# Halved searches, a regrouped last sum of experts and a re-ordered last norm in a one-core transformer kernel

## The chip, the core and the metric

The kernel runs on one core of a Trainium2 chip. The metric is the device time of one execution in microseconds (us); times of a kernel are given as the median of several executions. The profile is that of one execution. The engines are TensorE (PE, with its weight loads as PEld), VectorE (DVE), ScalarE (ACT), GpSimd (POOL) and SyncE (SP), each with a queue of its own that is worked off in order; DMAs are issued from the queues of SP, ACT and POOL.

## The reference

Two residual blocks over 256 tokens of width 1024, in float32. The change lies in the second block's last part, a feed-forward layer with 16384 small experts (PEER), and in the norm that ends the model:

```
q = (hc @ w_query).reshape(B, T_CHUNK, PEER_HEADS, 2, PEER_DKEY // 2)
s = jnp.einsum('bthpd,hpnd->bthpn', q, sub_keys)
s_top, i_top = lax.top_k(s, PEER_TOPK)                 # 16 of 128 keys, for 8 heads and 2 halves
cand = s_top[..., 0, :, None] + s_top[..., 1, None, :]
g_s, pos = lax.top_k(cand, PEER_TOPK)                  # 16 of the pairs: an expert each
g = jax.nn.softmax(g_s, axis=-1)
act = jax.nn.gelu(jnp.einsum('btd,bthkd->bthk', hc, u_emb[e_idx]))
y = jnp.einsum('bthk,bthkd->btd', g * act, v_emb[e_idx])
...
x = x + g2[:, None, :] * y
return rms_norm(x, norm_final)     # x * rsqrt(mean(x*x) + EPS) * g
```

## The kernel before, in words

Tokens lie in two tiles of 128 (t = 0, 1), `xt[t]`; the normed input stands transposed in `hT`. Matmuls keep float32's precision with three passes: every operand is split into a high part, by ScalarE (`whi`, L157), and the rest, by VectorE (`wlo`, L137), and `mm3` (L207 to L209) multiplies high by high, low by high and high by low. The third pass is the one that needs `wlo`. Weights come through SP's queue into `raw`, in the fixed order of the list `items`; `nextw` hands out the next one and has the splits made two ahead in this part (`cfg["ahead"]` = 2).

The expert layer doesn't gather. It treats the 16384 experts as 128 groups of 128, here called experts 0 to 127. `s_step` makes the scores of one such expert for all tokens: 24 matmuls of 128x256 into the bank `sm`, in two halves of 12, then a gelu on ScalarE into `act`. A weight of each token for each expert is made as a product of one-hot matrices, and the sum over all experts is added up in four PSUM banks `po[t][h]`, h being the half of 512 columns. It runs in these stages:

- The key search. `top16` takes the 16 largest of each row with VectorE's MAX, MAX_INDEX and MATCH_REPLACE; one job is a block of 4 scores of 128 keys. Six of eight jobs run beside the query projections; the last two are the first thing in `route`. `route` is a generator that writes VectorE's work and yields a number after each piece. `keep_up` adds up these numbers and writes one `s_step` for each 1.6 of them behind the piece, so this sets the order in which `wlo` of the experts' weights stand between the pieces of VectorE's queue. Behind the route stand the transposes of its results `fl`.
- The one-hot blocks. 34 steps (`bt`) over 32 blocks of 8 tokens: `g_onehot` (VectorE: `oh` L1475, then the product `a` L1477), `g_mm` (PE, 24 matmuls, L1488) one step later, `g_out` (ScalarE, L1497). Some `s_step` are spread evenly over the steps; how many depends on how many were made in the route (`left`). Within a step the block's matmuls stand between the two halves of an `s_step`.
- The sum. `quanta` is the list of PE's work: remaining `s_step`, and for each expert n its two token tiles. `w_step(n)` multiplies scores by weights (VectorE `wf`, L1538) and splits the product (`wh` on ScalarE, L217, `wl` on VectorE, L218); it is written two experts ahead of its use. A tile of an expert is 6 matmuls of 128x512, three for each h.
- The end. `gated` multiplies a finished bank with the row `g2` and adds it to x (L1080, L1081 of `Gated`), then ScalarE sums the squares (L279). `rms` adds two sums (L1593) and GpSimd takes the power -0.5 (L1594). `give` multiplies x with this column and the norm's weight row `gf` in one VectorE instruction (L1598) and stores the half (L1599).

Of the kernel before, what the change touches and what calls it, by code (L numbers as in the profile page):

```python
# [9 lines left out]
F32 = mybir.dt.float32  # L10
# [4 lines left out]
AF = mybir.ActivationFunctionType  # L15
OP = mybir.AluOpType
# [3 lines left out]
P = 128  # L20
D = 1024
S = 256
NT = S // P
NEG = -1e30
USED = -3e38
EPS = 1e-6
# [3 lines left out]
NE = 128  # L30
# [30 lines left out]
def kernel(ctx: ExitStack, tc: tile.TileContext, A, LAY, stop=None):  # L61
    nc = tc.nc
    ctx.enter_context(tc.manual_schedule())
    V, ACT, G, PE = nc.vector, nc.scalar, nc.gpsimd, nc.tensor

    def pool(name, bufs=1, **kw):
        return tc.tile_pool(name=name, bufs=bufs, reuse_waits="tile", **kw)
# [5 lines left out]
    def pmm():  # L73
        return ps.tile([P, 512], F32, name="mm", tag="mm", bufs=4)
# [7 lines left out]
    def small(shape, name, dt=F32, bufs=4):  # L82
        return cst.tile(shape, dt, name=name, tag=name, bufs=bufs)

    def row(ap, n=D, eng=None):
        r = cst.tile([P, n], F32, name="grow", tag="grow", bufs=2)
        (eng or G).dma_start(r, bass.AP(tensor=ap.tensor, offset=ap.offset, ap=[[0, P], [1, n]]))
        return r
# [5 lines left out]
    xt = [cst.tile([P, D], F32, name=f"x{t}") for t in range(NT)]  # L94
# [70 lines left out]
    def nextw():  # L165
        while items[st["use"]][3] is not None:
            st["use"] += 1
        j = st["use"]
        ahead, k = 0, j + 1
        while k < len(items) and ahead < cfg["ahead"] and not cfg["spread"]:  # L170
            ahead += items[k][3] is None
            k += 1
        while st["split"] < k:
            split_one()
        while st["s"][j].lo is None:
            low_one()
        st["use"] += 1
        return st["s"].pop(j), items[j][1], items[j][2]
# [27 lines left out]
    def mm3(out, a, b, start, stop):  # L206
        PE.matmul(out, a[0], b[0], start=start, stop=False)  # L207
        PE.matmul(out, a[0], b[1], start=False, stop=False)  # L208
        PE.matmul(out, a[1], b[0], start=False, stop=stop)  # L209
# [68 lines left out]
    def sumsq(src, out, scale=1.0):  # L278
        ACT.activation(junk[:, :src.shape[1]], src, AF.Square, scale=scale, accum_out=out)  # L279
# [377 lines left out]
    for i in range(4):  # L657
        n = len(items)
# [24 lines left out]
    for x_ in seq:  # L683
        n = cnt[x_]
# [46 lines left out]
    for i in range(4):  # L731
        c, nk, _ = nextw()
# [133 lines left out]
    with pool("df") as sp:  # L866
# [3 lines left out]
        v = sp.tile([P, NT, D], F32, name="v")  # L870
        qx = sp.tile([P, 4, S], F32, name="xq")
        q = [sp.tile([P, 4, S], F32, name="q", tag=f"q{b}", bufs=1) for b in range(2)]
        k = [sp.tile([P, 4, S], F32, name="k", tag=f"k{b}", bufs=1) for b in range(2)]
# [403 lines left out]
    def top16(jobs):  # L1277

        for r in range(2):
            a, b = 8 * r, 8 * r + 8  # L1280
            for v_, i_, src in jobs:
                V.max(v_[:, a:b], src)  # L1282
            for v_, i_, src in jobs:
                V.max_index(i_[:, a:b], v_[:, a:b], src)  # L1284
            if r == 0:
                for v_, i_, src in jobs:
                    V.match_replace(src, v_[:, a:b], src, USED)  # L1287
# [72 lines left out]
    def s_step():  # L1360
        n = len(act)
        u, _, _ = nextw()
        p = psm()[:, :S]
        early = n % (AHEAD + 2) < FIRST
        act[n] = (dp if early else apool).tile([P, S], F32, name="act", tag="act", bufs=FIRST if early else AHEAD + 2 - FIRST)
        for k in range(8):
            mm3(p, u[:, k, :], hT[:, k, :], k == 0, k == 7)
            if k == 3:
                yield
        ACT.activation(act[n], p, AF.Gelu)  # L1370
        yield
# [8 lines left out]

    def route():
        for j_ in jobs:
            top16(j_)
            yield 4.0
        ib, gs, pos, fl = [], [], [], []
        for t in range(NT):
            ib.append(pq2.tile([P, 2, P, 2], BF16, name="ib", tag="ib", bufs=2))
# [28 lines left out]
            for s_ in range(2):  # L1416
                e = pq2.tile([P, 8, 16, 16], BF16, name="eq", tag="eq", bufs=2)
                V.tensor_tensor(e, io16[:, None].to_broadcast([P, 8, 16, 16]), pab[:, s_, :, None, :].to_broadcast([P, 8, 16, 16]),
                                op=OP.is_equal)
# [37 lines left out]
    for dt in route():  # L1457
        keep_up(dt)
# [62 lines left out]
    gpool = gst.enter_context(pool("gr"))  # L1521
    GW = {}

    def g_load(b):

        GW[b] = gpool.tile([P, NG, GI, GT], F32, name="G", tag="G", bufs=2)
        nc.scalar.dma_start(GW[b], gall[:, :, GI * GT * b:GI * GT * (b + 1)].rearrange("g p (i t) -> p g i t", t=GT))
# [5 lines left out]
    po = [[pmm() for h in range(2)] for t in range(NT)]  # L1533
    W = {}

    def w_step(n):
        wf = gpool.tile([P, S], F32, name="wf", tag="wf", bufs=3)
        V.tensor_tensor(wf.rearrange("p (g t) -> p g t", t=GT), act[n].rearrange("p (g t) -> p g t", t=GT), GW[n // GI][:, :, n % GI, :],  # L1538
                        op=OP.mult)
        W[n] = Split(gpool.tile([P, S], F32R, name="wh", tag="wh", bufs=3), gpool.tile([P, S], F32R, name="wl", tag="wl", bufs=3))  # L1540
        split_evac(W[n][:, :], wf)

    quanta = [("u", None)] * (2 * (AHEAD - len(act)))
    pos_ = AHEAD
    for n in range(NE):
# [2 lines left out]
            pos_ += 1  # L1548
        pos_ += 1
        quanta += [("v", (n, 0)), ("v", (n, 1))]  # L1550
    quanta[-4:] = [("v", (n, t, [h])) if t else ("v", (n, t)) for t, h in ((0, 0), (1, 0), (1, 1)) for n in (NE - 2, NE - 1)]
    vs = {}
    half = None
    for i, (kind, arg) in enumerate(quanta):
        if quanta[i + 1:i + 2] == [("v", (0, 0))]:
            w_step(0)
            w_step(1)
        if kind == "u":
            if half is None:
                half = s_step()  # L1560
                next(half)
            else:
                next(half)
                half = None
            continue
        n, t = arg[:2]
        if t == 0:
            if n == NE // 2:
                g2 = row(gdram[1], eng=nc.sync)
                gb2 = row(A["b_ada_2"][0, 5120:6144], eng=nc.sync)  # L1570
            if n == NE // 2 + 8:
                V.tensor_tensor(g2, g2, gb2, op=OP.add)
                gf = row(A["norm_final_2"], eng=nc.sync)
            vs[n], _, _ = nextw()
            if n + 2 < NE:
                w_step(n + 2)
            if n % GI == 1 and n // GI + 1 < NE // GI and n // GI:
                g_load(n // GI + 1)
        for h in arg[2] if t and len(arg) > 2 else range(2):
            mm3(po[t][h], W[n][:, t * P:(t + 1) * P], vs[n][:, 0, h * 512:(h + 1) * 512], n == 0, n == NE - 1)  # L1580
        if t and n < NE - 2:
            W.pop(n), vs.pop(n)

    gate = Gated(g2)
    fss = small([P, NT, 2], "ssn", bufs=2)
    fr = small([P, NT], "fr", bufs=1)

    def gated(t, h):
        gate(t, h, po[t][h])
        sumsq(xt[t][:, h * 512:(h + 1) * 512], fss[:, t, h:h + 1], D ** -0.5)  # L1590

    def rms(t):
        V.scalar_tensor_tensor(fr[:, t:t + 1], fss[:, t, :1], EPS, fss[:, t, 1:], op0=OP.add, op1=OP.add)  # L1593
        G.tensor_tensor(fr[:, t:t + 1], fr[:, t:t + 1], mhalf[:, :1], op=OP.pow)  # L1594

    def give(t, h):
        c = slice(h * 512, (h + 1) * 512)
        V.scalar_tensor_tensor(xt[t][:, c], xt[t][:, c], fr[:, t:t + 1], gf[:, c], op0=OP.mult, op1=OP.mult)  # L1598
        nc.sync.dma_start(A["out"][0, t * P:(t + 1) * P, c], xt[t][:, c])  # L1599

    for f in ((gated, 0, 0), (gated, 0, 1), (gated, 1, 0), (rms, 0), (gated, 1, 1), (give, 0, 0), (rms, 1), (give, 0, 1),
              (give, 1, 0), (give, 1, 1)):
        f[0](*f[1:])


# [66 lines left out]
def build(nc, arrays, lay, stop=None):  # L1672
    aps = {n: nc.dram_tensor(f"in_{n}_dram", a.shape, mybir.dt.from_np(a.dtype), kind="ExternalInput").ap()
           for n, a in arrays.items()}
    aps["out"] = nc.dram_tensor("out_0_dram", (1, S, D), F32, kind="ExternalOutput").ap()
    with tile.TileContext(nc) as tc:
        kernel(tc, aps, lay, stop)
# [11 lines left out]
```

## Time and profile before

| | us |
|---|---|
| median of 3 executions | 2079.52 (2077.22 to 2084.33) |
| the profiled execution | 2077.22 |
| its span | 2075.4 |
| PE busy in it | 2022.7 (97%) |
| VectorE busy | 1451.7 (70%) |
| ScalarE busy | 990.9 (48%) |

The span is what the profile covers; the execution's time has something around it. Times within a view count from the span's start. The search of the route begins at 1286.08, the one-hot blocks reach from 1400 to 1540, and the last update of x begins at 2062.98. [...]

### The profile page before, as it was taken

Reading aid. Unit: us, or ns where it says so; the run is one execution under the profiler, and the core shown is the slowest. Engines: PE = TensorE matmul, PEld = TensorE weight load, DVE = VectorE, ACT = ScalarE, POOL = GpSimd, SP = SyncE. Lnnn points to the kernel's source line nnn. Section 1 sums busy time; section 2 is a strip of 40 time slices with the busy share of each in tenths; the row PEclk is TensorE's granted clock in tenths of the full one; section 3 lists DMA queues with packets and bytes.
Section 4 is the critical chain, followed back from the end, with each engine's and each line's share of the span. In section 5 each row is a group of like instructions: output and inputs, shape, how many; then the busy total and the mean of one; then the engine's idle time right before and its main releaser. Section 6 shows DMA issues by size and latency. Waiting matters only on the chain. (4 is left out here: it accounts for less than half of the span.)

```text
span 2075.4 us, 34428 instructions
## 1 busy us (share of the span) xinstructions
PE 2022.7 (97%) x13678; PEld 1819.8 (88%) x13678; DVE 1451.7 (70%) x2280; ACT 990.9 (48%) x1524; POOL 41.7 (2%) x74
## 2 busy tenths in 40 slices
PE   8999999999999999999999899999999999999998
PEld 7999888998899798899978778999998888888886
DVE  6677566776577559766556879889976666666666
ACT  6444354444344445454444544455554444444443
POOL 2000000000000000000000000000000000000000
PEclk9999999999999999999999999999999999999999
DMA  7667545666576643365635343556676676776764
GB/s 277 208 249 251 180 146 192 237 241 238 189 252 231 235 156 121 124 213 195 211 117 175 102 162 114 182 175 231 244 255 216 209 231 208 226 251 212 230 212 135
DMA packets 142377, 416.92 MB, mean 201 GB/s; under 512 B 12468, under 2 KB 47428, under 8 KB 140040
## 3 DMA queue, kind: packets, MB, share of 16 engines
q1 hardware_dynamic: 102672, 372.04, 53.0%
q10 hardware_dynamic: 37976, 36.91, 5.6%
q0 software_dynamic: 1568, 5.77, 0.9%
q8 instruction: 107, 1.75, 0.3%
q14 instruction: 54, 0.44, 0.1%
HBM read 396.82 MB, written 17.86 MB: 200 GB/s over the span
## 5 line engine op out<-in xcount | busy, mean ns | idle before, releaser
L137 DVE TENSOR_TENSOR wlo<-raw,whi 128x1024 fp32r<-128x1024 f32 (+1 forms) x654 | 784.7, 1222 | 331.1 <-ACT whi L157 330.5
L157 ACT ACTIVATE whi<-raw 128x1024 fp32r<-128x1024 f32 (+1 forms) x654 | 666.2, 1048 | 134.7 <-PE mm L209 68.1
L209 PE MATMUL mm<-hT_hi,wlo 128*128 128x256 f32 x1680 | 472.1, 281 | 8.8 <-DVE wlo L137 8.8
L207 PE MATMUL mm<-hT_hi,whi 128*128 128x256 f32 x1680 | 477.9, 284 | 0.0
L208 PE MATMUL mm<-hT_lo,whi 128*128 128x256 f32 x1680 | 471.3, 281 | 0.0
L209 PEld LDWEIGHTS mm<-hT_hi,wlo 128*128 128x128 f32 x1680 | 316.5, 188 | 10.2 <-DVE wlo L137 10.2
L207 PEld LDWEIGHTS mm<-hT_hi,whi 128*128 128x128 f32 x1680 | 316.8, 189 | 6.2 <-issue 5.5
L208 PEld LDWEIGHTS mm<-hT_lo,whi 128*128 128x128 f32 x1680 | 316.8, 189 | 2.0 <-issue 1.9
L207 PE MATMUL sm<-hT_hi,whi 128*128 128x256 f32 (+1 forms) x1048 | 299.6, 286 | 4.3 <-DVE hT_hi L215 2.5
L209 PE MATMUL sm<-hT_hi,wlo 128*128 128x256 f32 (+1 forms) x1048 | 296.4, 283 | 4.3 <-DVE wlo L137 4.3
L208 PE MATMUL sm<-hT_lo,whi 128*128 128x256 f32 (+1 forms) x1048 | 296.3, 283 | 0.4 <-DVE hT_lo L218 0.4
L207 PEld LDWEIGHTS sm<-hT_hi,whi 128*128 128x128 f32 (+1 forms) x1048 | 199.2, 190 | 7.5 <-DVE hT_hi L215 2.9
L207 PE MATMUL mm<-whi,wh 128*128 128x512 f32 x512 | 202.6, 396 | 2.7 <-ACT wh L217 2.7
L209 PEld LDWEIGHTS sm<-hT_hi,wlo 128*128 128x128 f32 (+1 forms) x1048 | 199.2, 190 | 4.7 <-DVE wlo L137 4.7
L208 PE MATMUL mm<-wlo,wh 128*128 128x512 f32 x512 | 202.3, 395 | 0.0
L209 PE MATMUL mm<-whi,wl 128*128 128x512 f32 x512 | 202.2, 395 | 0.0
L208 PEld LDWEIGHTS sm<-hT_lo,whi 128*128 128x128 f32 (+1 forms) x1048 | 199.0, 190 | 3.0 <-DVE hT_lo L218 0.6
L217 ACT ACTIVATE wh<-wf 128x256 fp32r<-128x256 f32 x128 | 53.5, 418 | 215.2 <-DVE wf L1538 215.2
L207 PE MATMUL mm<-whi,gT_hi 128*128 128x512 f32 x352 | 139.9, 397 | 0.0
L209 PE MATMUL mm<-whi,gT_lo 128*128 128x512 f32 x352 | 139.1, 395 | 0.0
L208 PE MATMUL mm<-wlo,gT_hi 128*128 128x512 f32 x352 | 139.0, 395 | 0.0
L1370 ACT ACTIVATE act<-sm 128x256 f32<-128x256 f32 x128 | 49.1, 384 | 167.3 <-PE sm L209 167.2
(308 smaller groups left out, 2597.7 us busy)
## 6 DMA issues: line engine op xcount, KB each, us to landing
raw<-in_ffn_up_dram SPq DMA_DIRECT2D x176, 512.0 KB, 5.1
raw<-in_peer_u_dram SPq DMA_DIRECT2D x128, 512.0 KB, 3.9
raw<-in_peer_v_dram SPq DMA_DIRECT2D x128, 512.0 KB, 3.6
raw<-in_ffn_dn_dram SPq DMA_DIRECT2D x88, 512.0 KB, 5.1
raw<-in_w_ada_dram SPq DMA_DIRECT2D x48, 512.0 KB, 4.7
gall<-stage ACTq DMA_DIRECT2D x16, 1024.0 KB, 4.8
G<-gall ACTq DMA_DIRECT2D x16, 1024.0 KB, 7.2
raw<-in_diff_w_in_dram SPq DMA_DIRECT2D x28, 512.0 KB, 4.4
```

Source lines behind the costliest of these rows:

```text
L137: V.tensor_tensor(lo[:, :nk * w], r[:, :nk * w], c.hi.rearrange("p k w -> p (k w)").bitcast(F32), op=OP.subtract)
L157: ACT.activation(hi[:, :n], r[:, :n], AF.Copy)
L207: PE.matmul(out, a[0], b[0], start=start, stop=False)
L208: PE.matmul(out, a[0], b[1], start=False, stop=False)
L209: PE.matmul(out, a[1], b[0], start=False, stop=stop)
L217: ACT.activation(hi, src, AF.Copy)
L1370: ACT.activation(act[n], p, AF.Gelu)
```

## The change

The route searches each of its two blocks in two halves of two jobs and yields 2.8 after each half, where it yielded 4.0 after a whole one. The last three experts, not the last two, are summed by token tile: tile 0 of all three, then the first half of tile 1 of all three, then its second half. At the end, x is multiplied with the norm's weight in a step of its own (`gain`) before the column is known, and `give` only scales by the column, the first half of each tile on VectorE and the second on ScalarE. The order of the steps is written anew, and the products have three tiles of their own.

```diff
     def route():
         for j_ in jobs:
-            top16(j_)
-            yield 4.0
+            for k in range(0, 4, 2):
+                top16(j_[k:k + 2])
+                yield 2.8
...
-    quanta[-4:] = [("v", (n, t, [h])) if t else ("v", (n, t)) for t, h in ((0, 0), (1, 0), (1, 1)) for n in (NE - 2, NE - 1)]
+    quanta[-6:] = [("v", (n, t, [h])) if t else ("v", (n, t)) for t, h in ((0, 0), (1, 0), (1, 1)) for n in range(NE - 3, NE)]
...
-        if t and n < NE - 2:
+        if t and n < NE - 3:
             W.pop(n), vs.pop(n)
 
-    gate = Gated(g2)
-    fss = small([P, NT, 2], "ssn", bufs=2)
+    tmp = [gpool.tile([P, 512], F32, name="tmp", tag="tmp", bufs=3) for _ in range(3)]
+    fss = small([P, NT, 2], "ssf", bufs=1)
     fr = small([P, NT], "fr", bufs=1)
-
-    def gated(t, h):
-        gate(t, h, po[t][h])
-        sumsq(xt[t][:, h * 512:(h + 1) * 512], fss[:, t, h:h + 1], D ** -0.5)
+    parts = {(0, 0): (0, 512), (0, 1): (512, 512), (1, 0): (0, 512), (1, 1): (512, 512)}
+
+    def gated(t, k):
+
+        c, w = parts[t, k]
+        m, x_ = tmp[(2 * t + k) % 3][:, :w], xt[t][:, c:c + w]
+        V.tensor_tensor(m, po[t][c // 512][:, c % 512:c % 512 + w], g2[:, c:c + w], op=OP.mult)
+        V.tensor_tensor(x_, x_, m, op=OP.add)
+        sumsq(x_, fss[:, t, k:k + 1], D ** -0.5)
...
+    def gain(t, k):
+        c, w = parts[t, k]
+        V.tensor_tensor(xt[t][:, c:c + w], xt[t][:, c:c + w], gf[:, c:c + w], op=OP.mult)
 
     def give(t, h):
         c = slice(h * 512, (h + 1) * 512)
-        V.scalar_tensor_tensor(xt[t][:, c], xt[t][:, c], fr[:, t:t + 1], gf[:, c], op0=OP.mult, op1=OP.mult)
+        if h:
+            ACT.activation(xt[t][:, c], xt[t][:, c], AF.Copy, scale=fr[:, t:t + 1])
+        else:
+            V.tensor_scalar(xt[t][:, c], xt[t][:, c], fr[:, t:t + 1], None, op0=OP.mult)
         nc.sync.dma_start(A["out"][0, t * P:(t + 1) * P, c], xt[t][:, c])
 
-    for f in ((gated, 0, 0), (gated, 0, 1), (gated, 1, 0), (rms, 0), (gated, 1, 1), (give, 0, 0), (rms, 1), (give, 0, 1),
-              (give, 1, 0), (give, 1, 1)):
+    for f in ((gated, 0, 0), (gated, 0, 1), (gain, 0, 0), (rms, 0), (gain, 0, 1), (gated, 1, 0), (give, 0, 0), (give, 0, 1),
+              (gated, 1, 1), (gain, 1, 0), (rms, 1), (gain, 1, 1), (give, 1, 0), (give, 1, 1)):
         f[0](*f[1:])
```

On VectorE, the first of the two searches of the route stood as follows before (`v` and `i` are the values and indices found, `sc` the scores):

```order
L1282 MAX v_12418<-sc 128x8 x4
L1284 MAX_INDEX i_12420<-v_12418,sc 128x8 x4
L1287 MATCH_REPLACE sc<-v_12418,sc 128x128 x4
L1282 MAX v_12418<-sc 128x8 x4
L1284 MAX_INDEX i_12420<-v_12418,sc 128x8 x4
L137 TENSOR_TENSOR wlo<-raw,whi 128x1024 x3
```

and in the changed kernel VectorE has in the same place, up to the end of the first half and its splits:

```order
L1282 MAX v_12418<-sc 128x8 x2
L1284 MAX_INDEX i_12420<-v_12418,sc 128x8 x2
L1287 MATCH_REPLACE sc<-v_12418,sc 128x128 x2
L1282 MAX v_12418<-sc 128x8 x2
L1284 MAX_INDEX i_12420<-v_12418,sc 128x8 x2
L137 TENSOR_TENSOR wlo<-raw,whi 128x1024 x2
```

The first `wlo` now stands behind two jobs instead of four. The pattern comes four times instead of twice, with 2, 2, 2 and 1 `wlo` behind it instead of 3 and 2; on PE 48 matmuls (two `s_step`) move from the one-hot blocks to the place ahead of the transposes of `fl`.

On VectorE among the one-hot blocks, around step 11 (`oh` are the one-hot matrices, `a` the products, `wlo` the rest of a split weight), before:

```order
L137 TENSOR_TENSOR wlo<-raw,whi 128x1024
L1475 TENSOR_TENSOR oh<-io_12986,iT 128x2048
L1477 TENSOR_TENSOR a_15234<-oh,gp 128x3072
L137 TENSOR_TENSOR wlo<-raw,whi 128x1024
L1475 TENSOR_TENSOR oh<-io_12986,iT 128x2048
L1477 TENSOR_TENSOR a_15300<-oh,gp 128x3072
```

and in the changed kernel:

```order
L137 TENSOR_TENSOR wlo<-raw,whi 128x1024
L1476 TENSOR_TENSOR oh<-io_12986,iT 128x2048
L1478 TENSOR_TENSOR a_15234<-oh,gp 128x3072
L1476 TENSOR_TENSOR oh<-io_12986,iT 128x2048
L1478 TENSOR_TENSOR a_15267<-oh,gp 128x3072
L137 TENSOR_TENSOR wlo<-raw,whi 128x1024
```

Before, a `wlo` stood between any two pairs of `oh` and `a`; here, and once more at step 22, it is gone together with its expert's 24 matmuls on PE.

On VectorE at the end (x_65 and x_66 are the token tiles 0 and 1, `grow` the rows `g2` and `gf`), from the update of the second half of tile 0 on, before:

```order
L1081 TENSOR_TENSOR x_65<-x_65,xg 128x512
L1080 TENSOR_TENSOR xg<-mm,grow 128x512
L1081 TENSOR_TENSOR x_66<-x_66,xg 128x512
L1593 SCALAR_TENSOR_TENSOR fr<-ssn 128x1
L1080 TENSOR_TENSOR xg<-mm,grow 128x512
L1081 TENSOR_TENSOR x_66<-x_66,xg 128x512
L1598 SCALAR_TENSOR_TENSOR x_65<-x_65,fr,grow 128x512
L1593 SCALAR_TENSOR_TENSOR fr<-ssn 128x1
L1598 SCALAR_TENSOR_TENSOR x_65<-x_65,fr,grow 128x512
L1598 SCALAR_TENSOR_TENSOR x_66<-x_66,fr,grow 128x512 x2
```

and in the changed kernel:

```order
L1595 TENSOR_TENSOR x_65<-x_65,tmp 128x512
L1604 TENSOR_TENSOR x_65<-x_65,grow 128x512
L1599 SCALAR_TENSOR_TENSOR fr<-ssf 128x1
L1604 TENSOR_TENSOR x_65<-x_65,grow 128x512
L1594 TENSOR_TENSOR tmp<-mm,grow 128x512
L1595 TENSOR_TENSOR x_66<-x_66,tmp 128x512
L1611 TENSOR_SCALAR x_65<-x_65,fr 128x512
L1594 TENSOR_TENSOR tmp<-mm,grow 128x512
L1595 TENSOR_TENSOR x_66<-x_66,tmp 128x512
L1604 TENSOR_TENSOR x_66<-x_66,grow 128x512
L1599 SCALAR_TENSOR_TENSOR fr<-ssf 128x1
L1604 TENSOR_TENSOR x_66<-x_66,grow 128x512
```

Three instructions of width 512 (two multiplications of x_65 with the weight and a scaling of it) now stand on VectorE between the update of tile 0 and the last update of x_66; before, only that of the first half of x_66 did. Two multiplications of x_66 and one scaling of it stand behind the last update, and two scalings have gone over to ScalarE's queue.

## Rows read from the trace of the kernel before

**Rows 1.** The page, part 1: busy time, share of the span, instructions.

```profile
PE 2022.7 (97%) x13678; PEld 1819.8 (88%) x13678; DVE 1451.7 (70%) x2280; ACT 990.9 (48%) x1524; POOL 41.7 (2%) x74
```

**Rows 2.** Waits of PE: line waited for: us in total, times, longest.

```profile
PE sm L209 <- DVE wlo L137: 4.3, 2, 3.8
```

**Rows 3.** Timeline of PE in the search: start, us, engine, line, operation [idle before].

```profile
1287.94 0.28 PE L208 MATMUL sm<-hT_lo,whi 128*128 128x256 f32 x1
1292.02 0.58 PE L209 MATMUL sm<-hT_hi,wlo 128*128 128x256 f32 x1 [3.80 <-DVE wlo L137]
...
1296.67 0.41 PE L209 MATMUL sm<-hT_hi,wlo 128*128 128x256 f32 x1
...
1297.06 0.28 PE L208 MATMUL sm<-hT_lo,whi 128*128 128x256 f32 x1
...
1299.91 0.28 PE L208 MATMUL sm<-hT_lo,whi 128*128 128x256 f32 x1
```

**Rows 4.** Timeline of VectorE in the same stretch.

```profile
1286.08 0.86 DVE L1282 MAX8 v<-sc 128x8 f32<-128x128 f32 x4
...
1290.75 3.49 DVE L137 TENSOR_TENSOR wlo<-raw,whi 128x1024 fp32r<-128x1024 f32 x3
```

**Rows 5.** Stretches of 0.5 us: busy by engine, then PE's granted clock (PEclk).

```profile
1290.00:1290.50 0.50, 0.00 (x0) 0.00 (x0) 0.50 (x6) 0.00 (x0) 0.00 (x0) 0.68 0.00 0
...
1297.00:1297.50 0.50, 0.50 (x6) 0.50 (x6) 0.50 (x4) 0.38 (x2) 0.00 (x0) 1.00 0.99 385
```

**Rows 6.** Timeline of VectorE: the products of one-hot blocks 11 and 22.

```profile
1446.08 1.76 DVE L1477 TENSOR_TENSOR a<-oh,gp 128x3072 bf16<-128x3072 bf16 x1
...
1493.74 1.76 DVE L1477 TENSOR_TENSOR a<-oh,gp 128x3072 bf16<-128x3072 bf16 x1
```

**Rows 7.** Timeline of PE: the matmuls of the same two blocks.

```profile
1450.87 1.32 PE L1488 MATMUL mm<-a,oh 128*128 128x128 bf16 x20
...
1498.29 1.55 PE L1488 MATMUL mm<-a,oh 128*128 128x128 bf16 x24
```

**Rows 8.** Timeline of PE at the end: experts 126 and 127, last matmul.

```profile
2058.91 0.50 PE L207 MATMUL mm<-whi,wh 128*128 128x512 f32 x1
...
2061.98 0.50 PE L207 MATMUL mm<-whi,wh 128*128 128x512 f32 x1 [1.41 <-ACT wh L217]
...
2066.04 0.39 PE L209 MATMUL mm<-whi,wl 128*128 128x512 f32 x1
```

**Rows 9.** Timeline of all engines at the end; SPq is SP's DMA queue.

```profile
2062.98 0.69 DVE L1080 TENSOR_TENSOR xg<-mm,grow 128x512 f32<-128x512 f32 x1 [0.59 <-PE mm L209]
2063.70 0.69 DVE L1081 TENSOR_TENSOR x<-x,xg 128x512 f32<-128x512 f32 x1
2064.32 0.68 DVE L1080 TENSOR_TENSOR xg<-mm,grow 128x512 f32<-128x512 f32 x1
...
2067.76 0.69 DVE L1081 TENSOR_TENSOR x<-x,xg 128x512 f32<-128x512 f32 x1
...
2069.14 3.19 SPq L1599 DMA_DIRECT2D out_dram<-x  x4
2069.29 0.16 DVE L1593 SCALAR_TENSOR_TENSOR fr<-ssn 128x1 f32<-128x1 f32 x1 [0.18 <-ACT junk L279]
2069.37 0.75 DVE L1598 SCALAR_TENSOR_TENSOR x<-x,fr,grow 128x512 f32<-128x512 f32 x1
...
2070.56 1.41 DVE L1598 SCALAR_TENSOR_TENSOR x<-x,fr,grow 128x512 f32<-128x512 f32 x2 [0.44 <-POOL fr L1594]
```

**Rows 10.** Groups by line and form: count, busy us, mean ns, idle before.

```profile
L363 DVE TENSOR_SCALAR hh<-x,r 128x512 f32<-128x512 f32 x2 | 2.2, 1110 | 1.5 <-POOL r L348 1.5
...
L363 DVE TENSOR_SCALAR hh<-hh,r 128x512 f32<-128x512 f32 x2 | 1.0, 487 | 1.3 <-POOL r L353 1.3
...
L364 ACT ACTIVATE hh<-hh,r 128x512 f32<-128x512 f32 x2 | 1.4, 724 | 2.3 <-POOL r L353 2.3
```

**Rows 11.** The page, part 6: KB of each, median us from issue to landing.

```profile
out_dram<-x SPq DMA_DIRECT2D x4, 256.0 KB, 2.0
```

More of the change, by code (lines that the diff above doesn't have):

```diff
@@ L1580 @@
             mm3(po[t][h], W[n][:, t * P:(t + 1) * P], vs[n][:, 0, h * 512:(h + 1) * 512], n == 0, n == NE - 1)
-        if t and n < NE - 2:
+        if t and n < NE - 3:
             W.pop(n), vs.pop(n)
-    gate = Gated(g2)
-    fss = small([P, NT, 2], "ssn", bufs=2)
+    tmp = [gpool.tile([P, 512], F32, name="tmp", tag="tmp", bufs=3) for _ in range(3)]
+    fss = small([P, NT, 2], "ssf", bufs=1)
     fr = small([P, NT], "fr", bufs=1)
-    def gated(t, h):
-        gate(t, h, po[t][h])
-        sumsq(xt[t][:, h * 512:(h + 1) * 512], fss[:, t, h:h + 1], D ** -0.5)
+    parts = {(0, 0): (0, 512), (0, 1): (512, 512), (1, 0): (0, 512), (1, 1): (512, 512)}
[5 more added lines that the diff above has]
+        sumsq(x_, fss[:, t, k:k + 1], D ** -0.5)
     def rms(t):
-        V.scalar_tensor_tensor(fr[:, t:t + 1], fss[:, t, :1], EPS, fss[:, t, 1:], op0=OP.add, op1=OP.add)
+        V.scalar_tensor_tensor(fr[:, t:t + 1], fss[:, t, :1], EPS, fss[:, t, 1:2], op0=OP.add, op1=OP.add)
         G.tensor_tensor(fr[:, t:t + 1], fr[:, t:t + 1], mhalf[:, :1], op=OP.pow)
+    def gain(t, k):
+        c, w = parts[t, k]
+        V.tensor_tensor(xt[t][:, c:c + w], xt[t][:, c:c + w], gf[:, c:c + w], op=OP.mult)
     def give(t, h):
         c = slice(h * 512, (h + 1) * 512)
-        V.scalar_tensor_tensor(xt[t][:, c], xt[t][:, c], fr[:, t:t + 1], gf[:, c], op0=OP.mult, op1=OP.mult)
+        if h:
+            ACT.activation(xt[t][:, c], xt[t][:, c], AF.Copy, scale=fr[:, t:t + 1])
+        else:
+            V.tensor_scalar(xt[t][:, c], xt[t][:, c], fr[:, t:t + 1], None, op0=OP.mult)
         nc.sync.dma_start(A["out"][0, t * P:(t + 1) * P, c], xt[t][:, c])
-    for f in ((gated, 0, 0), (gated, 0, 1), (gated, 1, 0), (rms, 0), (gated, 1, 1), (give, 0, 0), (rms, 1), (give, 0, 1),
-              (give, 1, 0), (give, 1, 1)):
+    for f in ((gated, 0, 0), (gated, 0, 1), (gain, 0, 0), (rms, 0), (gain, 0, 1), (gated, 1, 0), (give, 0, 0), (give, 0, 1),
+              (gated, 1, 1), (gain, 1, 0), (rms, 1), (gain, 1, 1), (give, 1, 0), (give, 1, 1)):
         f[0](*f[1:])
```

## The prediction

> **What bounds the kernel now.** I read the page first: TensorE (PE) is busy for 97% of the span [rows 1]. Work of another engine beside a running PE therefore costs nothing; time is to be won only where PE stands still or runs slowly, and behind its last matmul. The waits of PE say where it stands still. The longest that the change touches is 3.8 us for `wlo` [rows 2], in the key search. The timeline shows it: PE's last matmul there starts at 1287.94 and takes 0.28, the next starts at 1292.02 [rows 3]. VectorE meanwhile runs one search of four score blocks, from 1286.08, and makes the awaited `wlo` only at 1290.75 [rows 4]. The gap costs a second time. [...] The other stretch is the end. The view of all engines there shows VectorE at work almost without pause from 2062.98 until it waits for the square sum at 2069.29 and for the root at 2070.56 [rows 9]. There VectorE sets the end, not PE.
>
> **The search in halves.** A whole search takes 1290.75 - 1286.08 = 4.67 us [rows 4], a half, with every instruction of it present half as often, 2.33. From the start of `wlo` to PE's restart it is 1292.02 - 1290.75 = 1.27. With `wlo` behind the first half PE restarts at 1286.08 + 2.33 + 1.27 = 1289.68, so the gap is 1.46 instead of 3.80: 2.34 us won. If the gap stays shorter than the time at which the clock fell, the slow matmuls go too. In 1290.00 to 1290.50 the mean is 0.68 [rows 5], so full speed lasted 0.18 us into that slice: the fall came 1.96 us after PE stopped at 1288.22. A gap of 1.46 has ended by then, and one of 1.41 near the end left the matmuls at their usual pace [rows 8]. The 22 slow matmuls take 1296.67 - 1292.02 = 4.65 us for 21 steps; at full speed 24 steps take 1299.91 - 1297.06 = 2.85, so 21 take 2.49 [rows 3]. That is 2.16 us more, together **4.50 us won**. What is late next: a half search and two `wlo` are 2.33 + 2 x 1.2 = 4.7 us of VectorE (three `wlo` take 3.49 [rows 4]), against 2 x 2.85 = 5.7 us in which PE sums two experts, so PE stays the slower one. Outer ends: nothing won (then the wait is not the search's), or 3.80 + 2.16 = 5.96 if the rest of the gap goes as well.
>
> **Two experts move.** The yields of the search add up to 4 x 2.8 = 11.2 instead of 8.0, which at 1.6 an expert puts two more score sums, 48 matmuls, ahead of the transposes, and takes two out of the 34 steps with one-hot blocks. PE pays 2 x 2.85 at one place and saves it at the other. But the blocks of steps 11 and 22 lose the expert whose 2.85 us covered VectorE's making of the next one-hot. At block 11 VectorE's product is done at 1446.08 + 1.76 = 1447.84 [rows 6], PE begins the block at 1450.87 [rows 7], and would begin 2.85 earlier, at 1448.02: 0.18 is left. At block 22 it is 1495.50 [rows 6] against 1498.29 - 2.85 = 1495.44 [rows 7], a wait of 0.06. I take **0.1 us lost**. PE does not wait at these blocks now, so nothing can be won; with no slack at all VectorE, which saves one `wlo` of 1.2, would be 2.85 - 1.2 = 1.65 late at each, 3.3 in all.
>
> **The last three experts.** Their products still come through VectorE and ScalarE in the old order. PE waits for that of expert 127 until 2061.98 [rows 8], and token tile 0 needs this one, so its sums are ready no earlier than now. What changes is the filler: the six matmuls of expert 125 for tile 1 run no longer before the gap but behind it. PE's 18 last matmuls start within 2066.04 - 2061.98 = 4.06, 0.239 a step [rows 8], so six put PE's end off by **1.43**, from about 2066.4 to 2067.9. That counts only if VectorE would take the last sums sooner.
>
> **The scaling at the end.** One update of a half is two steps, 0.72 and 0.62 (2062.98, 2063.70, 2064.32) [rows 9]. Now four follow each other and the last add starts at 2067.76. After the change the order is: two updates, to 2065.66; one multiplication with the weight (0.62 by the pace above, 0.69 by itself), to 2066.28; the sum for the root, which comes 2069.29 - 2067.76 = 1.53 after an add starts [rows 9], hence at 2065.04 + 1.53 = 2066.57, and 0.08 for it (2069.29 to 2069.37); the second multiplication, to 2067.27; an update of tile 1, to 2068.61; one scaling by a column, 0.49 by itself [rows 10] and 0.42 as a step, since 0.69 by itself is a step of 0.62, to 2069.03; only then the last update, whose add starts at 2069.75. That is 2.0 us later than now, and later than PE's 2067.9, so PE's delay hides behind VectorE. The root's input follows at +1.53 = 2071.28 and the root at 2070.56 - 2069.29 = 1.27 after it [rows 9]: 2072.55. Both multiplications of tile 1 fit into these 2.8 us. Then the two scalings run side by side, 0.49 on VectorE and 0.72 on ScalarE [rows 10], where now two on VectorE take 1.41 [rows 9]. Compute ends at 2073.27 against 2070.56 + 1.41 = 2071.97: 1.3 later. The four stores are issued within 3.19 us from 2069.14 [rows 9], so the last issue takes place from about 2072.0 to 2072.3, and each lands 2.0 us after [rows 11]. The last two will follow each other more closely than now and may share the queue, up to 0.4 more. I take **1.6 us lost**. Ends: the column scaling has a second row, 1.11 on average of two [rows 10], which would add 0.6 to the highest, 1.3 + 0.4 + 0.6 = 2.3; the lowest is 0.8, if the waits for the first sum and the issue close up.
>
> **The sum** is -4.5 + 0.1 + 1.6 = -2.8 us. The profiled execution took 2077.22 (span 2075.4, the rest around it); with the change it would take 2074.4. The median of the three runs, 2079.52, is 2.3 above the profiled one, so I forecast 2076.7.
>
> [...] The new order at the end has PE stop twice. Now the twelve matmuls of expert 125 reach almost up to expert 126, which starts when its product comes, at 2058.91 [rows 8]; with six of them gone PE stands still for six steps there, 1.4 us, and after six matmuls another 1.41 before expert 127. In the search a single gap of 3.80 lowered the granted clock [rows 3, 5]. [...]
>
> **Rivals** (times on the median's scale).
> - *The end costs nothing.* For it: VectorE stands 0.4 us at the root and ScalarE is mostly free. Against: VectorE gets more work ahead of the last add, with no pause to hold it. -4.5 + 0.1: 2075.1.
> - *The clock still falls in the shortened gap.* For: the fall came late in the old one and the new one is three quarters as long as that took. Against: 1.41 and no fall. 2.16 comes back: 2078.9.
> - *The search is not what PE waits for*, so the halves do nothing. For: ScalarE's `whi` lies ahead of every `wlo`. Against: `wlo` follows the search without a pause on VectorE. -2.8 + 4.5: 2081.2.
> - *The clock falls at the end.* At half speed 21 steps took 4.65 instead of 2.49, 1.87 times as long; 12 matmuls of 0.239 a step then add 2.5 to PE's end, 2070.4, of which 1.4 comes out behind VectorE's need at 2069.0: 2078.1. For: the two gaps close together. Against: neither is as long as the one in the search was when the clock fell.
> - *Slower than before: the one-hot blocks become VectorE's.* At blocks 11 and 22 PE waits 1.65 each, and each wait lowers the clock and costs 2.16 more, as in the search: 2 x 3.8 = 7.6 in place of 0.1, so +4.7 and 2084.2. It begins to count when the product comes more than 0.2 us later than now against PE's block, and beats the gain from 1.5 us at each. For: the slack of 0.18 and -0.06. Against: VectorE's own order ahead of these products is unchanged.
>
> **How the numbers follow.** Forecast 0.55, no cost at the end 0.14, clock still falling in the search 0.08, no effect of the halves 0.06, clock at the end 0.09, one-hot blocks 0.08. The likeliest alone, with the bounds of the search and of the end and the spread of the runs shown (2077.22 to 2084.33), reaches from 2073.5 to 2080. For 8 in 10 I take **2072 to 2082**, which takes in all cases but the slowest. A difference of 0.3%, 6.2 us, is about what a measurement of this kernel can tell from none: faster means below 2073.3, slower above 2085.8. Forecast and first rival reach below 2073.3 with a fifth to a third of their chance, and a search that wins all of 5.96 adds some: faster 0.22. Slower takes most of the one-hot rival together with a high median: 0.05. Same 0.73.
>
> **What would show it.** Search: PE's gap at 1288 is 1.3 to 1.6 us, the granted clock stays 1.00 until 1300, and the next matmuls are 0.12 apart. One-hot: no wait above 0.3 at the two blocks. End, counted from VectorE's first update: the last add starts 6.8 after it (4.8 now), the two last scalings start 9.6 after (7.6 now), and the span ends about 14 after (12.4 now); PE's two gaps are 1.4 each. A gap in the search that stays near 3.8, or an end no longer than now, would make the prediction wrong.

## The result and the profile after

The changed kernel takes 2060.19 us (median of 6, 2056.94 to 2063.47) against 2081.11 for the kernel before (6 runs, 2077.22 to 2084.33): a ratio of 0.990 with an interval of 0.9887 to 0.9913. The forecast was 2076.7, and its range ended at 2072. The change wins 20.9 us where 2.8 were forecast; the profiled execution took 2063.47, with a span of 2061.4.

The page after says little of it: PE is busy for 13.2 us less than before [rows 1], with as many instructions.

```profile
PE 2009.5 (97%) x13678; PEld 1824.4 (88%) x13678; DVE 1451.8 (70%) x2282; ACT 992.0 (48%) x1526; POOL 42.0 (2%) x74
```

The places that the prediction spoke of look as it said. In the search (timeline of PE; answers to [rows 3]) the gap is 1.59 us where 1.46 was worked out:

```profile
1284.64 0.28 PE L208 MATMUL sm<-hT_lo,whi 128*128 128x256 f32 x1
1286.50 0.39 PE L209 MATMUL sm<-hT_hi,wlo 128*128 128x256 f32 x1 [1.59 <-DVE wlo L137]
1286.73 0.28 PE L207 MATMUL sm<-hT_hi,whi 128*128 128x256 f32 x1
1286.85 0.28 PE L208 MATMUL sm<-hT_lo,whi 128*128 128x256 f32 x1
```

Before, the granted clock was 0.50 from 1290.18 to 1297.00, 1.00 being full speed, and the matmuls in that stretch were 0.21 apart. Now it stays at 1.00 there (last columns of the stretches: clock, DMA share, GB/s; compare [rows 5]), and the matmuls behind the gap are 0.12 apart:

```profile
1286.00:1286.50 0.50, 0.00 (x0) 0.00 (x0) 0.50 (x2) 0.05 (x1) 0.00 (x0) 1.00 0.00 0
1286.50:1287.00 0.50, 0.50 (x4) 0.50 (x5) 0.50 (x1) 0.00 (x0) 0.00 (x0) 1.00 0.00 0
```

At the two one-hot blocks (products of VectorE, matmuls of PE; [rows 6, 7]) PE begins 0.06 us after the product is done, at 1444.14 + 1.76 = 1445.90 and 1488.44 + 1.76 = 1490.20. Two blocks with half an expert's matmuls between them start 2.85 apart where nothing is waited for (1440.24 to 1443.09). Against this PE loses next to nothing at the first (1445.96 - 1443.09 = 2.87) and 0.2 at the second (1490.26 - 1487.19 = 3.07):

```profile
1440.24 1.55 PE L1489 MATMUL mm<-a,oh 128*128 128x128 bf16 x24
...
1443.09 1.55 PE L1489 MATMUL mm<-a,oh 128*128 128x128 bf16 x24
1444.14 1.76 DVE L1478 TENSOR_TENSOR a<-oh,gp 128x3072 bf16<-128x3072 bf16 x1
1445.96 1.55 PE L1489 MATMUL mm<-a,oh 128*128 128x128 bf16 x24
...
1487.19 1.55 PE L1489 MATMUL mm<-a,oh 128*128 128x128 bf16 x24
...
1488.44 1.76 DVE L1478 TENSOR_TENSOR a<-oh,gp 128x3072 bf16<-128x3072 bf16 x1
1490.26 1.55 PE L1489 MATMUL mm<-a,oh 128*128 128x128 bf16 x24
```

And the end (timeline of all engines, some rows left out; compare [rows 9]):

```profile
2043.34 0.51 PE L207 MATMUL mm<-whi,wh 128*128 128x512 f32 x1 [1.41 <-ACT wh L217]
...
2046.42 0.50 PE L207 MATMUL mm<-whi,wh 128*128 128x512 f32 x1 [1.42 <-ACT wh L217]
...
2047.43 0.69 DVE L1594 TENSOR_TENSOR tmp<-mm,grow 128x512 f32<-128x512 f32 x1 [0.60 <-PE mm L209]
...
2053.54 4.67 SPq L1612 DMA_DIRECT2D out_dram<-x  x4
...
2054.14 0.69 DVE L1595 TENSOR_TENSOR x<-x,tmp 128x512 f32<-128x512 f32 x1
...
2056.89 0.72 ACT L1609 ACTIVATE x<-x,fr 128x512 f32<-128x512 f32 x1 [1.23 <-POOL fr L1600]
2056.89 0.48 DVE L1611 TENSOR_SCALAR x<-x,fr 128x512 f32<-128x512 f32 x1 [0.44 <-POOL fr L1600]
```

PE's two gaps are 1.41 and 1.42. From VectorE's first update at 2047.43 the last add comes 6.71 later (6.8 forecast), the last two scalings 9.46 (9.6), and the span, which the profile gives to a tenth, ends 14.0 after it (about 14; before 12.4).

None of this makes 20 us. The rest shows only when a stretch is compared in which neither code nor order changed, the sums of experts. The next two fences give the same place in PE's timeline, before and after:

```profile
1699.98 0.39 PE L207 MATMUL mm<-whi,wh 128*128 128x512 f32 x1
1700.22 0.40 PE L208 MATMUL mm<-wlo,wh 128*128 128x512 f32 x1
1700.45 0.39 PE L209 MATMUL mm<-whi,wl 128*128 128x512 f32 x1
1700.68 0.40 PE L207 MATMUL mm<-whi,wh 128*128 128x512 f32 x1
...
1702.08 0.40 PE L207 MATMUL mm<-whi,wh 128*128 128x512 f32 x1
```

```profile
1699.82 0.39 PE L207 MATMUL mm<-whi,wh 128*128 128x512 f32 x1
1700.05 0.39 PE L208 MATMUL mm<-wlo,wh 128*128 128x512 f32 x1
1700.27 0.39 PE L209 MATMUL mm<-whi,wl 128*128 128x512 f32 x1
1700.50 0.39 PE L207 MATMUL mm<-whi,wh 128*128 128x512 f32 x1
...
1701.86 0.39 PE L207 MATMUL mm<-whi,wh 128*128 128x512 f32 x1
```

No wait, clock 1.00, the same instructions; but nine steps (from the start of a matmul to the start of the next) take 2.10 us before and 2.04 after, 0.233 and 0.227 each. Of a matmul's two operands, one is loaded ahead as weights (the rows of PEld: 128x128, 0.19 us each, in the stretch above started 0.23 us ahead of their matmul's row), and the other, here called the moving one, has the 512 or 256 columns that give the matmul its width. Over all rows of the traces, the 128x512 steps whose weights are `wh` and `wl` (the experts), `gT` or `cat` (sums of earlier layers) have a mean of 0.2333 before and 0.2270 after. There are 2880 of them (1536 with `wh` and `wl`, 1056 with `gT`, 288 with `cat`): an estimate of 2880 x 0.0063 = 18.1 us. Nothing in the profile names a cause. The compiled programs differ in one thing that reaches these stages: the new tile `ssf`, which takes 32 bytes in the pool `cst`, stands ahead of them in SBUF, where all these tiles lie, so each tile of a later pool starts 32 bytes further on. `whi` and `wlo`, here the moving operands, stay (start 224 modulo 256 bytes); the operands loaded as weights go from 192 to 224.

### The profile page after: what moved, and what is told of

It reads as the page before. It is cut to its first block, busy times and chain, and to the rows that moved or that the text cites. A ratio compares the mean times of both kernels' runs of the same rounds, so it can differ in the third digit from the quotient of the medians.

```text
span 2061.4 us, 34431 instructions
## 1 busy us (share of the span) xinstructions
PE 2009.5 (97%) x13678; PEld 1824.4 (88%) x13678; DVE 1451.8 (70%) x2282; ACT 992.0 (48%) x1526; POOL 42.0 (2%) x74
```

## The experiments

Theory A is that this move of 32 bytes made the gain; theory B that the named edits did. All unused tiles below are only allocated; no instruction touches them. Steps are means over the PE rows of a trace, of matmuls that directly follow one of the same width, from 50 us on; steps above 0.28 us (512 wide) or 0.14 us (256 wide), in which PE waits or runs at the lower clock (0.50), are left out. The kernel before was run again beside each group of experiments, with medians of 2079.3 to 2081.5; ratios are to these.

**e1 to e4: the move alone, and the edits without it.**

```diff
     # e1: 32 bytes (e2: [P, 16], 64 bytes), in the kernel before
+    small([P, 8], "pad", bufs=1)
     fr = small([P, NT], "fr", bufs=1)

     # e3, in the changed kernel
-    fss = small([P, NT, 2], "ssf", bufs=1)
+    fss = small([P, NT, 2], "ssn", bufs=2)

     # e4, in the kernel before: 32 bytes ahead of the weights' pools
+    ctx.enter_context(pool("pad", side="right")).tile([P, 8], F32, name="pad", tag="pad", bufs=1)
     wpool = ctx.enter_context(pool("wp", side="right"))
```

> The kernel before with one unused column tile of 32 bytes added where the changed kernel has ssf; nothing else differs, every tile allocated behind it moves by 32 bytes. Theory A (place in SBUF: the 512-wide matmul takes 0.227 a step where both of its operands start at 32 modulo 64 bytes, 0.233 where one starts at 0 and the other at 32): about 2880 matmuls gain 0.0067 each, so 2081.1 - 19 = 2062, and the step of the expert sums is 0.227. Theory B (the named edits made the gain): 2081, step 0.233.

> The kernel before with an unused column tile of 64 bytes at the same place: every tile behind it moves, but its start modulo 64 bytes stays. Theory A (remainder by 64 bytes decides): 2081, step of the expert sums 0.233. Rival A2 (any other place would do, as some clash of particular addresses goes away): 2062, step 0.227. Theory B: 2081.

> The changed kernel with the square sums of the last norm in the old tag ssn again, so that no tile is added ahead of the others and all starts modulo 64 bytes are those of before; all edits of the change stay. Theory A: step 0.233 again, and what is left is the predicted sum of the parts, -2.8: 2078. Theory B: 2060.

> The kernel before with 32 unused bytes ahead of the weight pools, so that the split weights (whi, wlo) start at 0 modulo 64 bytes like all the operands they meet, instead of at 32. Theory A as relative (the two operands of a matmul need the same remainder): step 0.227 in the expert sums and also where hT is the partner, so 2081 - 19 - 1.4 = 2060 or less, the more if the 256-wide step of 0.1185 falls too. Theory A as absolute (the operand loaded as weights has to be at 32): 2081 and 0.233.

e1 took 2060.37, ratio 0.9902 (0.9887 to 0.9917): one unused tile gives as much as the whole change. e2 took 2080.58, 0.9992 (0.9983 to 1.0001): no change. e3, all edits without the tile, took 2078.70, 0.9987 (0.9978 to 0.9996), 2.8 below before. e4 took 2041.14, 0.9807 (0.9794 to 0.9820). Theory B falls. One row per kernel shows the pace: PE's instructions from 1600 to 2000 us, where only expert sums and scores run (first pair behind the length: PE busy and count). Before, e1, e2, e3 and e4 in turn:

```profile
1600.00:2000.00 400.00, 400.00 (x2223) 345.61 (x2223) 250.86 (x343) 194.16 (x284) 0.00 (x0) 1.00 0.71 226
```

```profile
1600.00:2000.00 400.00, 400.00 (x2267) 352.56 (x2267) 255.70 (x348) 197.95 (x291) 0.00 (x0) 1.00 0.72 226
```

```profile
1600.00:2000.00 400.00, 400.00 (x2226) 346.18 (x2225) 250.87 (x342) 194.33 (x285) 0.00 (x0) 1.00 0.71 226
```

```profile
1600.00:2000.00 400.00, 400.00 (x2223) 345.59 (x2222) 250.83 (x343) 194.19 (x284) 0.00 (x0) 1.00 0.73 226
```

```profile
1600.00:2000.00 400.00, 400.00 (x2276) 352.68 (x2275) 256.82 (x349) 198.72 (x293) 0.00 (x0) 1.00 0.73 230
```

PE is full in all five and does 2223 to 2276 instructions in the same 400 us. In e4 the 256-wide step fell as well, from 0.1185 to 0.1154; those steps multiply `hT` (moving) by `whi` and `wlo` (weights), of which there are some 8150, so by an estimate (8150 x 0.0031) 25 of its 40 us come from there.

**e5, e6, e8: the edits where the operands lie well.** e5 is e3 with e4's line, e6 the kernel before with e4's line and the search in halves alone. e8 is e6 with another end, in which only the last quarter of x gets the change's `gain` and its scaling on ScalarE:

```diff
-        V.scalar_tensor_tensor(xt[t][:, c], xt[t][:, c], fr[:, t:t + 1], gf[:, c], op0=OP.mult, op1=OP.mult)
+        if t and h:
+            ACT.activation(xt[t][:, c], xt[t][:, c], AF.Copy, scale=fr[:, t:t + 1])
+        else:
+            V.scalar_tensor_tensor(xt[t][:, c], xt[t][:, c], fr[:, t:t + 1], gf[:, c], op0=OP.mult, op1=OP.mult)
...
     ... (give, 0, 0), (rms, 1), (give, 0, 1),
-              (give, 1, 0), (give, 1, 1)):
+              (gain, 1, 1), (give, 1, 0), (give, 1, 1)):
```

> The changed kernel without the added tile ssf (square sums in ssn again) and with 32 unused bytes ahead of the weight pools, as in e4. All edits of the change stay. Theory A: what the edits are worth by themselves (-2.8 as forecast) adds to the 2041.1 of e4: 2038.3, with the step of the expert sums at 0.227. Rival: the edits are worth nothing or harm once PE is faster, as VectorE comes later against it: 2041 or more.

> The kernel before with the 32 unused bytes ahead of the weight pools and with the search in halves (yields of 2.8) alone; sums of the last experts and the end as before. Forecast of the parts: -4.4 (gap and clock of the search, less 0.1 at the one-hot blocks) from 2041.1: 2036.7, so 1.6 below e5, and the span from VectorE's first update to the end stays at 12.4. Rival (the halves are worth nothing): 2041.1, and the 1.6 of the end shows as a gain of e5.

> e6 with another end: order of before, but the last quarter (second half of tile 1) is multiplied with the weight on VectorE while the second root is awaited, and scaled by the column on ScalarE beside VectorE's scaling of the third quarter. Forecast: VectorE has room for one more multiplication of 0.62 before the root comes (it waits 0.44 there now and the multiplication may end as late as the root), so the end moves up by the 0.7 of one scaling: 2036.0. Rival: the stores of the last two quarters, issued together, share the queue and nothing is gained: 2036.7.

e5: 2041.18 (ratio 0.9810, 0.9795 to 0.9825), no gain over e4. e6: 2038.55 (0.9799, 0.9786 to 0.9812), 2.6 below e4. e8: 2039.76 (0.9805, 0.9791 to 0.9818), no gain over e6. These differences are within the intervals; the traces are finer. From VectorE's first update to the end of the span it is 12.4 in e4 and e6, 12.5 in e8 and 14.0 in e5. So the change's end costs 1.6, and e8's end wins nothing: it finishes computing 0.4 sooner (8.55 after the first update instead of 8.99), but the stores take that back, as its rival said: their last issue moves up by 0.1 and the end of the span not at all.

In the search the faster PE waits longer than in the changed kernel (1.59 us): 2.13 in e6, 2.21 in e5 and 2.23 in e8. The prediction's second rival, the clock that falls all the same, comes true in two of the three. In e6 the granted clock (the number behind the five engines) falls to 0.50 as the gap ends. In e5 it is still 1.00 when PE restarts at 1270.51, and falls at 1272.00. In e8, with the longest of these gaps, it stays at 1.00. Rows of e6, of e5 and of e8:

```profile
1268.50:1269.00 0.50, 0.42 (x2) 0.42 (x3) 0.50 (x2) 0.00 (x0) 0.00 (x0) 0.55 0.00 0
```

```profile
1270.50:1271.00 0.50, 0.49 (x4) 0.49 (x5) 0.50 (x1) 0.00 (x0) 0.00 (x0) 1.00 0.00 0
...
1272.00:1272.50 0.50, 0.50 (x5) 0.50 (x4) 0.50 (x5) 0.00 (x0) 0.00 (x0) 0.50 0.80 295
```

```profile
1267.50:1268.00 0.50, 0.50 (x5) 0.50 (x6) 0.50 (x1) 0.00 (x0) 0.00 (x0) 1.00 0.00 0
1268.00:1272.00 4.00, 4.00 (x36) 4.00 (x35) 4.00 (x19) 1.33 (x2) 0.00 (x0) 1.00 0.80 247
```

So the times of e5 and e6 both contain a fall of the clock, and the length of a gap alone does not tell whether one comes. Two kernels below with the unhalved search say the same: both have a gap of 3.56 us there, and the clock falls behind it in e11 (restart 1292.32, first row) and not in e13 (restart 1301.15, second row):

```profile
1294.00:1294.50 0.50, 0.50 (x5) 0.50 (x4) 0.50 (x2) 0.00 (x0) 0.00 (x0) 0.50 0.86 311
```

```profile
1302.00:1310.00 8.00, 8.00 (x69) 8.00 (x68) 8.00 (x36) 2.82 (x5) 0.00 (x0) 1.00 0.61 200
```

**e7, e9, e10: is it the remainder by 64?** e7 is e4 with e1's line too; e9 has e1's line ahead of `hT` instead; e10 is e4 with e2's 64 bytes.

```diff
     # e9
+    small([P, 8], "pad", bufs=1)
     hT = Split(cst.tile([P, 8, S], F32R, name="hT_hi"), cst.tile([P, 8, S], F32R, name="hT_lo"))
```

> The kernel before with 32 unused bytes ahead of the weight pools and 32 in the place of ssf: split weights and hT start at 0 modulo 64 bytes, the operands wh, wl, gT and cat at 32. Relative theory (equal remainders): the step of the expert sums goes back to 0.233 and that of 256 wide stays at 0.1155: 2041.1 + 18 = 2059. Absolute theory (operand loaded as weights at 32 is good, whatever the other is): step 0.227, 2041.

> The kernel before with 32 unused bytes ahead of hT instead of ahead of the weight pools: the split weights keep their start at 32 modulo 64 bytes and every operand that they meet, hT too, moves to 32. Relative theory (equal remainders, whichever): 512-wide steps 0.227, 256-wide ones 0.115, 2041 as in e4. Rival (both at 0 is the good case for the 256-wide): 2060 as in e1.

> e4 with 64 further unused bytes where ssf stood, so that the tiles behind it move against the weights and hT by 64. e7, where they had moved by 32, had its 256-wide steps at 0.114 against 0.1155 in e4 although hT and the weights lay as in e4. If the remainder by 64 is all that counts: as e4, 2041 with 0.1155. If the place of other tiles modulo more than 64 bytes decides on the 256-wide step: up to 8160 x 0.0013 = 10 less or as much more, 2031 to 2051.

e9 took 2041.81 (0.9829, 0.9812 to 0.9847), as e4 with its 2041.14: not the remainder itself but the relation of the two operands counts. e7 took 2048.71 (0.9857, 0.9840 to 0.9873), between its two forecasts: the 512-wide step went back to 0.2332 as the relative theory says, but the 256-wide one, whose operands had not moved against e4, fell from 0.1154 to 0.1142. e10 took 2055.92 (0.9884, 0.9869 to 0.9900), outside what either side gave it: its 512-wide step is 0.2332. So the remainder by 64 that I had in mind is not the rule.

**e11, e13 to e16: which difference is good?** All are e4 with two unused tiles in `cst`, one ahead of `hT` and one where `ssf` stood: 64 and 192 bytes (e11), 64 and 64 (e13), 192 and 64 (e14), 128 and 128 (e15), 32 and 224 (e16). e12 is e11 with the search in halves.

```diff
+    small([P, 16], "pad1", bufs=1)
     hT = Split(cst.tile([P, 8, S], F32R, name="hT_hi"), cst.tile([P, 8, S], F32R, name="hT_lo"))
...
+    small([P, 48], "pad2", bufs=1)
     fr = small([P, NT], "fr", bufs=1)
```

> The kernel before with unused bytes alone: 32 ahead of the weight pools, 64 ahead of hT and 192 where ssf stood. In all runs so far the 512-wide step was 0.227 where the operand loaded as weights and the moving one started at the same remainder by 256 bytes, 0.230 where the former lay 64 lower, 0.233 at differences of 32, 64 and 224; the 256-wide was 0.1154 at a difference of 64 and 0.1183 at 96, and never stood at 0. Here nearly all stand at 0. If equal remainders are the good case for both widths: 256-wide 0.1133 (half of 0.2267), so 8148 x 0.0022 = 18 and 2 for hT below e4: 2021. Rival (the 256-wide has its own limit): as e4, 2039.

> e11 with 64 instead of 192 bytes where ssf stood: hT and the weights as in e11, but the 2880 operands wh, wl, gT and cat lie 128 off the weights. If the remainder by 128 decides: as e11, step of the expert sums 0.227. If that by 256: 0.233 there and 19 more than e11.

> As e11, with hT so placed that the split weights start 128 above it by 256 bytes (192 and 64 unused bytes); wh, wl, gT and cat stay level with the weights. If only nearness does harm (0 the worst, 64 the good side): 256-wide step 0.1155 or less, 2041 or less. If the step rises again away from 64: 0.118 to 0.120, 2061 to 2077.

> As e14 with a difference of 192, the mirror image of e4's 64 (128 and 128 unused bytes). If the distance alone counts: 256-wide step 0.1155, 2041. If its sign counts: 0.118 to 0.120, 2061 to 2077.

> As e14 with a difference of 32 (32 and 224 unused bytes), between the worst seen at 0 (0.1198) and the best at 64 (0.1155). If the step goes evenly with the difference: 0.1177, 2059. If every odd multiple of 32 is like the 96 of the kernel before: 0.1184, 2064.

> e11 with the search in halves, the one part of the change that the traces show to gain (gap of 1.6 instead of 3.8, no fall of the clock): 2.6 below e11, as e6 was below e4. Rival: with a faster PE the one-hot blocks, which lose an expert each, wait for VectorE, and nothing is left of it.

e11 took 2072.83 (0.9963, 0.9949 to 0.9977), far outside both its forecasts: of the differences measured, level operands are the best case for the 512-wide matmul (0.2273 in the table below) and the worst for the 256-wide one, at 0.1198; my theory fell. e13 took 2086.70 (1.0030, 1.0019 to 1.0042), 13.9 above e11, with 0.2324 where the operands lie 128 apart: the remainder by 128 does not decide. e14 took 2066.74 (0.9928, 0.9912 to 0.9945), e15 2059.82 (0.9900, 0.9879 to 0.9922; outside both its forecasts), e16 2066.10 (0.9930, 0.9914 to 0.9947): for the 256-wide step neither distance alone nor an even slope holds, but 32 is like 96 (0.1183 each; 0.1154 at 64, 0.1175 at 192). e12 took 2069.56 (0.9946, 0.9932 to 0.9960), 3.3 below e11, near the 2.6 expected. All traces together, by the start of the operand loaded as weights less that of the moving one, modulo 256 bytes (us a step; the 512-wide cells at 160 and 192 come from matmuls with `hT` as weights):

| difference | 0 | 32 | 64 | 96 | 128 | 160 | 192 | 224 |
|---|---|---|---|---|---|---|---|---|
| 512 wide | 0.2273 | 0.2332 | 0.2332 | | 0.2324 | 0.2335 | 0.2296 | 0.2333 |
| 256 wide | 0.1199 | 0.1183 | 0.1154 | 0.1183 | 0.1189 | | 0.1175 | |

The kernel before had 224 and 96; the change moved the first to 0 and left the second; e4 and e9 have 0 and 64, the best of each row. The fastest version is e6, that place with the halved search: 2038.55, 42 below the kernel before and 22 below the changed one.

## Why the prediction was wrong

The parts were sized rightly, and the sum of what they touch came out: -2.8 forecast, -2.8 measured in e3, where the edits stand alone. Its interval allows -0.8 to -4.6, so that the two agree to the tenth is luck.

- *The search in halves.* Gap 1.46 forecast, 1.59 measured, clock at 1.00: the number held. Its reason, that the slow matmuls go once the gap ends sooner than the 1.96 us after which the clock had fallen, is not borne out: in e5 (gap of 2.21) and e11 (3.56) the clock fell only after PE had restarted, while the longer gap of e8 (2.23) and the equal one of e13 (3.56) had no fall. Why like gaps act differently is not shown. The three traces with gaps of 1.24 to 1.59 (e12, e3, the changed kernel) show no fall there; how much of that is luck no run here shows.
- *Two experts move.* 0.1 forecast, 0.2 measured, at the second block. The prediction did not look for the clock elsewhere in this stage: it falls to 0.50 for 3.4 us each at 1400.42 and at 1543.78 in the changed kernel and nowhere between 1300 and 2060 in the trace before, but e1, with none of the edits, has such a fall at 1540.63, so it is not shown that the edits cause them.
- *The last three experts.* PE's two gaps of 1.4 and its later end, hidden behind VectorE: held; the clock stayed at 1.00 from 2041 to 2052.
- *The end.* +1.6 forecast, 14.0 - 12.4 = +1.6 measured.
- *The sum.* This is the step that failed: "-4.5 + 0.1 + 1.6 = -2.8" takes every stage that the edits do not name at its old duration. It lacks a term, by the estimate above -18.1 for 2880 matmuls of 512 columns whose weights `ssf` moved by 32 bytes, and with it the sum is -20.9, the measured figure. The diff showed the new tag, and the prediction passes over it; none of my rivals had a mechanism that reaches unchanged code, so a range built from the rows of three places could not hold the result. Taken apart, e1's 21.1 and e3's 2.8 make 23.9; the 3 us to 20.9 lie within the intervals and are not explained further, so here too the agreement to the tenth is luck.

Why the pace depends on the difference is not settled: no trace shows a cause of the steps of 0.227 and 0.233 in the fences above.

In e1 the tiles of the other engines moved as well, and no run here moves PE's operands alone. But the traces tell the two apart. Taken only over steps beside which VectorE, ScalarE and GpSimd did nothing, from 0.1 us before the first start to 0.1 us behind the second, the 512-wide step has a mean of 0.2332 before (235 steps) and of 0.2267 in the changed kernel and in e1 (226 and 223), and the 256-wide one of 0.1185 before (401) and 0.1155 in e4 (321). So the difference is there where those three engines do nothing.

A second thing stays open: at the same difference of 64 the 256-wide step is 0.118 in e4's stage from 1600 us on and 0.114 in e7's. Beside idle engines (all such steps lie ahead of that stage) it is 0.1155 in e4 and 0.1154 in e7 (323 steps), so this second effect shows only where other engines work; what makes it is not shown.

## What to carry to other kernels

Here one added tile moved the tiles of the later pools by its 32 bytes; before costing the edits of a diff that adds a tile or changes a tag, compare the starts of the operands of the dominant instructions in both programs. When a result is larger than the sum of its parts, compare the step of instructions in a stretch that nobody edited; if it differs, test an unused tile of the same size in the old kernel first. In this kernel, with PE busy for 97% of the span, the place of weights against moving data was worth 40 us of 2081 (e4), and the good place differed with the width (a difference of 0 for 512 wide, 0.2273; of 64 for 256 wide, 0.1154), so it has to be measured for each.

## What was not expected of the hardware

With clock 1.00 and no wait, one and the same 128x512 matmul took 0.227 or 0.233 us a step, and a 128x256 one 0.114 to 0.120 on average, by where tiles lie. For the most part it was the place of the two operands towards each other that counted (e9, with the differences of e4 at starts 32 bytes further on, took 2041.81, e4 2041.14), and the difference was there beside idle engines too (0.2332 and 0.2267). A move by 32 bytes counted (21.1 us in e1), and one by 64 or 128 was not always neutral (0.2332 in e10 and 0.2324 in e13 against 0.2273 for level operands; in e2 a move by 64 changed nothing, 2080.58 against 2081.51). Busy shares did not show it: PE reads 97% before and after.
